# Stick-breaking attention: a block's cast behind the next block's sigmoids on ScalarE, and a fourth buffer for cast probabilities

## The chip, the cores and the metric

The kernel runs on one core of a Trainium2 chip. The metric is the device time of one execution in microseconds (us), as the median of several executions. Five engines work side by side, each through its own queue in order: TensorE (PE in the profile; PEld is its loading of weights), VectorE (DVE), ScalarE (ACT), GpSimd (POOL) and SyncE (SP), which here issues nearly all DMAs. An instruction that waits for a semaphore holds up whatever stands behind it on its engine.

## The reference

One layer of an encoder block with 2048 positions and 1024 columns, batch 1. A normalized input goes through one projection whose columns feed two kinds of attention: four heads of differential attention (two softmax maps each) and eight heads of stick-breaking attention. Both outputs are normalized, projected and added to the input; a gated feed-forward part follows. The part that the change touches is this, with `s < t` strictly:

```python
def stick_breaking_attention(q, k, v):
    """A[t,s] = beta_ts * prod_{s<j<t}(1 - beta_tj), s < t."""
    ...
        z = jnp.einsum('bqhd,bkhd->bhqk', qb, k).astype(jnp.float32) * scale
        log_1mb = jnp.where(mask, jax.nn.log_sigmoid(-z), 0.0)
        rem = lax.cumsum(log_1mb, axis=3, reverse=True) - log_1mb
        a = jnp.where(mask, jnp.exp(jax.nn.log_sigmoid(z) + rem), 0.0)
        return jnp.einsum('bhqk,bkhd->bqhd', a.astype(v.dtype), v)
```

There is no softmax: each weight is a sigmoid times the product of (1 - sigmoid) of all later keys before the query.

## The kernel before, in words

The work is cut into 8 head groups: groups 0 to 3 are one differential head each, groups 4 to 7 are two stick-breaking heads each (m = 0, 1). Queries go in 16 tiles of 128 rows (i), keys in blocks of up to 1024 columns (b) which are computed in chunks of up to 512 (c), the highest first. The projection of the next group (`proj_tile`, `proj_out`, `proj_batch`) is fed in between the attention tiles of the present one by `advance`, and in the last group the output projection (`out_proj`, `post`, `x_ops`) takes that place. The feed-forward part comes afterwards.

A 32-bit number that goes into a matmul is split into two 16-bit halves, high and low, and products take three matmuls. So each block of probabilities is split as well, and transposed by a DMA, since the keys have to lie on the partitions for the product with v.

One stick-breaking block (`stage_a`, L549 to L572) takes, for each chunk: scores on TensorE into a PSUM tile `sc` (L457, four such tiles); on ScalarE the sigmoid of -z into `om` (L563) and the sigmoid of z, `beta` (L566), into the PSUM tile itself or into the tile `be`; on VectorE a running product over the reversed columns (the scan, L568); and on VectorE or GpSimd the product of beta with the shifted scan (L569), which gives the block's probabilities in `be`. `be` and `om` come from the ring `z4` of ZB = 9 tiles (z in the profile). Which engine a part goes to is decided while the program is written out, by `pick`, which keeps a sum of estimated costs for each engine (`load`, `note`).

When the chunks are done, `split_t` (L407) does the split and the transposition:

- a buffer `s16` of 2048 half-precision columns (s in the profile) is taken from a ring of SB = 3; the softmax half uses the same ring, and so does `post` for the operands of the feed-forward part,
- the high half is a cast by `to16`: on ScalarE for stick-breaking (L89),
- the low half is a subtraction (`tt`, L98): on GpSimd for stick-breaking,
- the transposing DMA is issued by SyncE (L412) into `aT`, a ring of AB = 5.

`stage_b` then multiplies the transposed block by v (`pv`, L467), PD = 5 blocks later. An s16 buffer is free when the transpose has landed.

The order on each engine is not the order of the text alone: a scheduler lays out all instructions at build time by priority, by a simulated course of time and by free buffers, and the result is fixed. `queue_behind` (L209) adds edges without a semaphore: an instruction is to stand behind another one on the same engine. So far only the feed-forward part uses it.

The tile `st` (two buffers) holds the split queries and keys before they are transposed, with room for 6 columns of heads; `out_proj` uses the same tag for rows of x (1024 numbers of 32 bit).

Of the kernel before, what the change touches and what calls it, by code (L numbers as in the profile page):

```python
# [11 lines left out]
F32 = mybir.dt.float32  # L12
F16 = mybir.dt.float16
BF16 = mybir.dt.bfloat16
I32 = mybir.dt.int32
AF = mybir.ActivationFunctionType
# [5 lines left out]
S, D, P = 2048, 1024, 128  # L22
# [13 lines left out]
KW = {"A": 1.0, "D": 1.0, "P": 1.0}  # L36
AHEAD = 2
AHN = 0
QB, KB, ZB, AB, SB, PD = 4, 7, 9, 5, 3, 5
XL = (0, 4, 5, 2, 1, 6, 3)  # L40
CU = 3
WE = "AP"
# [17 lines left out]
def block(tc, a, out):  # L60
    nc = tc.nc
    PE, ACT, DVE, POOL, SP = nc.tensor, nc.scalar, nc.vector, nc.gpsimd, nc.sync
    top = ExitStack()
    with top:
# [16 lines left out]
        def level():  # L81
            for k in load:
                load[k] = 0.0

        def to16(dst, src, n, engines="ADP", psum=False):
            cost = {"A": 0.84 * n + 110, "D": (1.05 if psum else 0.53) * n + 70, "P": 1.1 * n + 80}
            e = pick(**{k: cost[k] for k in engines})
            if e == "A":
                ACT.copy(dst, src)  # L89
            elif e == "D":  # L90
                DVE.tensor_copy(dst, src)
            else:
                POOL.tensor_scalar(dst, src, 1.0, 0.0, op0=ALU.mult, op1=ALU.add)
# [15 lines left out]
        def nm(s):  # L109
            uid[0] += 1  # L110
            return f"{s}{uid[0]}"
# [97 lines left out]
        def queue_behind(later, first):  # L209
            for z in later:  # L210
                tc.add_manual_dep(z.ins, first.ins.name, mybir.DependencyInfo(mybir.DependencyClass.NoSync, mybir.DependencyReason.DATA), reason="issue order")
# [46 lines left out]
        pp = pjs.enter_context(tc.tile_pool(name="pp", bufs=2, side="right"))  # L258

        with ExitStack() as ph1:  # L260
# [127 lines left out]
            def proj(g, G, fresh=None):  # L388
                for t in range(NT):
                    if fresh is not None:  # L390
                        feed(t)
                        xt = ahead.pop(0)
                    else:
                        xt = pp.tile([P, 2 * D], F16, tag="xt", bufs=3, name=nm("xt"))
                        SP.dma_start(xt[:], xs[t])
                    if t % 4 == 0:
                        st = pp.tile([P, 6, 4, 2, 64], F16, tag="st", name=nm("st"))
                        v = sp.tile([P, 4, 256], F16, tag="v", bufs=KB, name=nm("v"))
                        raw = pp.tile([P, 4, 256], F32, tag="raw", name=nm("raw")) if g < 4 else None
                    pj = proj_tile(G, xt)  # L400
                    proj_out(g, G, pj, (st, v, raw), t % 4)
                    if t % 4 == 3:
                        proj_batch(g, G, (st, v, raw))
                    yield

            @pri("spl")
            def split_t(src, n, he="ADP", le="DP"):  # L407
                s16 = s16p.tile([P, 2048], F16, tag="s16", bufs=SB, name=nm("s16"))
                to16(s16[:, :n], src, n, he)
                tt(s16[:, n : 2 * n], src, s16[:, :n], ALU.subtract, n, le)  # L410
                aT = sp.tile([P, 16, P], F16, tag="aT", bufs=AB, name=nm("aT"))
                SP.dma_start_transpose(aT[:, : 2 * n // P, :], s16[:, : 2 * n])  # L412
                return aT
# [129 lines left out]
                values(*prev)  # L543

            def sb_attn(g, G):
                last = {}

                @pri("at")
                def stage_a(i, m, b):  # L549
                    L = (i + 1) * 128  # L550
                    n = min(1024, L - 1024 * b)
                    be, om = z4(), z4()
                    if b == i // 8:
                        DVE.memset(om[:, n : n + 1], 8192.0)
                    else:
                        DVE.tensor_copy(om[:, n : n + 1], last[m][:, 0:1])
                    last[m] = om
                    for c in range((n - 1) // 512, -1, -1):
                        lo, hi = 512 * c, min(512 * c + 512, n)
                        w = hi - lo  # L560
                        sc = ps.tile([P, 512], F32, tag="sc", bufs=4, name=nm("sc"))
                        score_chunk(G, sc, i, 2 * b + c, m, w // P, b == i // 8 and hi == n)
                        ACT.activation(om[:, lo:hi], sc[:, :w], AF.Sigmoid, scale=G["nkz"][:])  # L563
                        e = pick(D=1.04 * w + 155, P=2.4 * w + 100)
                        beta = sc[:, :w] if e == "D" else be[:, lo:hi]
                        ACT.activation(beta, sc[:, :w], AF.Sigmoid, scale=G["kz"][:])  # L566
                        ov = om[:, lo:hi][:, ::-1]
                        DVE.tensor_tensor_scan(ov, ov, sc[:, :w], om[:, hi : hi + 1], op0=ALU.mult, op1=ALU.bypass)  # L568
                        (DVE if e == "D" else POOL).tensor_tensor(be[:, lo:hi], beta, om[:, lo + 1 : hi + 1], ALU.mult)  # L569
                        note("A", 1.7 * w + 400)  # L570
                        note("D", 2.08 * w + 200)
                    return n, split_t(be[:, :n], n, "A", "P")  # L572

                ypd = {}

                def stage_b(i, m, b, n, aT):
                    r, k = fq(g, i)
                    if i // k not in ypd:
                        ypd[i // k] = ps.tile([P, 512], F32, tag="yp", name=nm("yp"))
                    yp = ypd[i // k]  # L580
                    pv(G, yp, P * r + 64 * m, aT, b, n, 128 * m, 64, r == 0 and m == 0 and b == i // 8, r == k - 1 and m == 1 and b == 0)
                    if m == 1 and b == 0 and r == k - 1:
                        finish(g, G, i, k, yp)
                        G["fin"] = i + 1

                pend = []
                done = 0
                for i in range(NT):
                    if i % 4 == 0:
                        level()  # L590
                    for b in range(i // 8, -1, -1):
                        for m in range(2):
                            n, aT = stage_a(i, m, b)
                            pend.append((i, m, b, n, aT))
                            if len(pend) > PD:
                                stage_b(*pend.pop(0))
                            done += n // P + CS
                            yield done / (272 + 48 * CS), (i + 1 if b == 0 and m == 1 else i)
                for u in pend:
                    stage_b(*u)  # L600
# [154 lines left out]
            def out_proj():  # L755
                for t in range(NT):
                    mt = pp.tile([P, 2 * D], F16, tag="xt", bufs=3, name=nm("mt"))[:].rearrange("p (k n) -> p k n", k=KT)
                    with tc.high_priority(PRI["wm"]) if PRI["wm"] else nullcontext():
                        mts.append(SP.dma_start(mt, ms[t]))
                    if t in spare:  # L760
                        xf = spare[t].bitcast(F32)
                    else:
                        xf = pp.tile([P, 6, 4, 2, 64], F16, tag="st", name=nm("xf"))[:].rearrange("p c t s e -> p (c t s e)").bitcast(F32)[:, :D]
                    SP.dma_start(xf, x[t * P : (t + 1) * P, :])
                    for h in range(2):
                        po = psj.tile([P, 512], F32, tag="pj", name=nm("po"))
                        for n in range(2):
                            q = 0
                            sl = slice(256 * n, 256 * n + 256)
                            for kt in range(KT):  # L770
                                for xi, wi in ((0, 0), (0, 1), (1, 0)):
                                    PE.matmul(po[:, sl], lhsT=mt[:, kt, P * xi : P * xi + P], rhs=wos[2 * h + n][wi][:, kt, :], start=q == 0, stop=q == 23)  # L772
                                    q += 1
                            xl = xf[:, 512 * h + 256 * n : 512 * h + 256 * n + 256]
                            DVE.scalar_tensor_tensor(xl, po[:, sl], kos[2 * h + n][:], xl, op0=ALU.mult, op1=ALU.add)  # L775
                    note("D", 1400)
                    SP.dma_start(hd[t], xf)
                    if t >= 12:
                        yield
                        continue  # L780
                    post(t, xf)
                    yield
# [459 lines left out]
```

## Time and profile before

| | us |
|---|---|
| Median of 3 runs | 2723.46 (2717.96 to 2725.68) |
| The profiled execution | 2726.11 |
| Its span in the trace | 2724.3 |

The granted TensorE clock was 0.975 on the mean. A profile row of a group of instructions names line, engine, operation and tiles (`out<-in`), then count, busy time, mean duration and the idle time of the engine just before, with what ended it. A row of waits reads "who waited <- for whom: total us, times, longest us". In a row of a window of time stand its length, then the busy time of each engine with the number of instructions in brackets, the granted clock, the mean busy share of the 16 DMA engines, and GB/s. In a timeline each row has start, duration, engine, line and operation; square brackets tell how long the engine stood idle before it and what ended that.

### The profile page before, as it was taken

What the parts mean: (1) busy time and instruction counts of PE and PEld (TensorE: products, weight loads), DVE (VectorE), ACT (ScalarE), POOL (GpSimd) and SP (SyncE); (2) the same over time, 40 slices, a digit from 0 to 9 for tenths busy, and PEclk for the clock granted to TensorE, in tenths of its full rate; (3) what the DMA queues carried; (4) which work ended last, traced back from release to release, by engine and by line L of the source; (5) the groups of instructions that cost most, each with busy time, mean ns of one, the idle gap of its engine ahead of it and who ended that gap; (6) DMA issues with size and microseconds to landing.
All of it is one profiled execution on the core that took longest, in us unless ns stands there. A gap on an engine that the chain in (4) does not pass through costs nothing. (4 is left out here: it accounts for less than half of the span.)

```text
span 2724.3 us, 45559 instructions
## 1 busy us (share of the span) xinstructions
PE 2471.4 (91%) x17084; PEld 1404.6 (52%) x17084; DVE 1945.7 (71%) x3716; ACT 1345.8 (49%) x2483; POOL 1569.3 (58%) x1134
## 2 busy tenths in 40 slices
PE   7998989898888786779888999999999999999998
PEld 4655655555555453557775444444444444444443
DVE  6898979698888988876666877777786544444445
ACT  4665656567878878765644535444352112111121
POOL 2577767667767777765655666575674232323223
PEclk9999999999999997999999999999999999999999
DMA  6788797779999998996797675666749744545534
GB/s 223 205 168 176 149 195 161 177 170 206 208 207 203 205 183 159 205 202 199 203 268 266 237 245 201 220 215 212 251 170 350 279 175 145 224 151 190 208 125 166
DMA packets 649134, 551.92 MB, mean 203 GB/s; under 512 B 506624, under 2 KB 574208, under 8 KB 638672
## 3 DMA queue, kind: packets, MB, share of 16 engines
q1 hardware_dynamic: 647088, 546.92, 73.2%
q8 instruction: 134, 2.20, 0.3%
q0 software_dynamic: 512, 1.36, 0.2%
q10 hardware_dynamic: 1312, 0.72, 0.1%
q14 instruction: 88, 0.72, 0.1%
HBM read 265.27 MB, written 151.52 MB: 153 GB/s over the span
## 5 line engine op out<-in xcount | busy, mean ns | idle before, releaser
L329 PE MATMUL pj<-w,xt 128*128 128x384 f16 x3072 | 570.1, 333 | 26.3 <-DVE st L339 10.8
L98 POOL TENSOR_TENSOR s<-z,s 128x1024 f16<-128x1024 f32 (+7 forms) x288 | 477.5, 1667 | 99.3 <-ACT s L89 94.8
L329 PEld LDWEIGHTS <-xt 128*128 128x128 f16 x3072 | 298.5, 100 | 233.8 <-issue 38.2
L568 DVE TENSOR_TENSOR_SCAN z<-z,sc 128x512 f32<-128x512 f32 (+3 forms) x320 | 352.9, 1112 | 81.4 <-ACT sc L566 39.3
L1048 PE MATMUL pd<-wd,act 128*128 128x512 f16 x1848 | 405.3, 379 | 3.9 <-DVE hs L1054 2.4
L457 PE MATMUL sc<-kT,qT 128*128 128x512 f16 (+3 forms) x1280 | 339.6, 357 | 51.7 <-DVE z L568 16.2
L467 PE MATMUL yp<-v,aT 128*128 128x64 f16 (+1 forms) x4896 | 279.6, 207 | 91.5 <-DMA aT<-s 90.4
L467 PEld LDWEIGHTS <-aT 128*128 128x128 f16 x4896 | 242.2, 101 | 181.9 <-DMA aT<-s 120.2
L98 POOL TENSOR_TENSOR act<-cg,act 128x512 f16<-128x512 f32 x117 | 166.3, 1434 | 239.4 <-ACT act L1006 133.1
L950 PEld LDWEIGHTS <-wg 128*128 128x128 f16 x1848 | 181.1, 98 | 222.0 <-issue 7.9
L1048 PEld LDWEIGHTS <-act 128*128 128x128 f16 x1848 | 180.6, 98 | 222.7 <-issue 4.8
L950 PEld LDWEIGHTS <-wu 128*128 128x128 f16 x1848 | 181.9, 99 | 219.0 <-issue 6.5
L98 POOL TENSOR_TENSOR hs<-hs,cu 128x512 f32<-128x512 f32 x132 | 166.9, 1269 | 220.9 <-DVE hs L1054 76.0
L98 POOL TENSOR_TENSOR fst<-fst 128x512 f32<-128x512 f32 x97 | 182.6, 1883 | 161.3 <-DVE wd L224 89.9
L1054 DVE SCALAR_TENSOR_TENSOR hs<-pd,c,hs 128x512 f32<-128x512 f32 x192 | 141.6, 748 | 155.6 <-PE pd L1048 151.9
L89 ACT CAST s<-z 128x384 f16<-128x384 f32 (+7 forms) x216 | 171.6, 800 | 133.5 <-DMA aT<-s 104.5
L563 ACT ACTIVATE z<-sc,c 128x512 f32<-128x512 f32 (+3 forms) x320 | 207.0, 650 | 25.7 <-PE sc L457 18.5
L569 POOL TENSOR_TENSOR z<-z,z 128x512 f32<-128x512 f32 (+3 forms) x148 | 151.5, 1027 | 100.7 <-DVE z L568 85.6
L772 PE MATMUL po<-wo,mt 128*128 128x256 f16 x1536 | 180.1, 276 | 20.2 <-DVE xf L775 11.2
L1006 ACT CAST act<-cg 128x512 f16<-128x512 f32 x132 | 81.1, 616 | 218.1 <-DVE cg L1012 173.6
L950 PE MATMUL pm<-X,wg 128*128 128x512 f16 x792 | 179.7, 380 | 0.0
L950 PE MATMUL pm<-X,wu 128*128 128x512 f16 x792 | 179.4, 379 | 0.0
(237 smaller groups left out, 4139.3 us busy)
## 6 DMA issues: line engine op xcount, KB each, us to landing
xt<-xs SPq DMA_DIRECT2D x112, 512.0 KB, 4.2
hs<-hd SPq DMA_DIRECT2D x96, 512.0 KB, 4.4
hd<-hs SPq DMA_DIRECT2D x80, 512.0 KB, 4.4
split<-wg SPq DMA_DIRECT2D x11, 1792.0 KB, 11.3
split<-wu SPq DMA_DIRECT2D x11, 1792.0 KB, 10.4
split<-wd SPq DMA_DIRECT2D x11, 1792.0 KB, 10.5
wg<-split SPq DMA_DIRECT2D x11, 1792.0 KB, 7.2
wd<-split SPq DMA_DIRECT2D x11, 1792.0 KB, 8.9
```

What stands on the lines that cost most here:

```text
L89: ACT.copy(dst, src)
L98: (DVE if e == "D" else POOL).tensor_tensor(dst, a_, b_, op)
L329: PE.matmul(pj[:, :384], lhsT=xv[:, xi, kt, :], rhs=G["w"][:, wi, kt, :], start=n == 0, stop=n == 23)
L457: PE.matmul(sc[:, : 128 * w].rearrange("p (t n) -> p t n", n=P), lhsT=G["q"][i // 4][:, 2 - 2 * o + m, i % 4, :], rhs=G["k"][q][:, m, 0:w, ...
L467: PE.matmul(yp[:, y0 : y0 + wd], lhsT=aT[:, a_, :], rhs=v[:, v_ : v_ + wd], start=start and j == 0 and q == 0, stop=stop and j == nb - 1 a ...
L563: ACT.activation(om[:, lo:hi], sc[:, :w], AF.Sigmoid, scale=G["nkz"][:])
L568: DVE.tensor_tensor_scan(ov, ov, sc[:, :w], om[:, hi : hi + 1], op0=ALU.mult, op1=ALU.bypass)
L569: (DVE if e == "D" else POOL).tensor_tensor(be[:, lo:hi], beta, om[:, lo + 1 : hi + 1], ALU.mult)
L772: PE.matmul(po[:, sl], lhsT=mt[:, kt, P * xi : P * xi + P], rhs=wos[2 * h + n][wi][:, kt, :], start=q == 0, stop=q == 23)
L950: PE.matmul(ps_[:].rearrange("p (t n) -> p t n", n=P), lhsT=wv[:, wo, wi, 128 * kt : 128 * kt + 128], rhs=X[xo][:, :, xi, kt, :], start=st ...
L1048: PE.matmul(po[:], lhsT=act[:, ao, xi, 128 * j : 128 * j + 128], rhs=W["d"][:, wo, wi, :], start=start and u == 0 and q == 0, stop=u == nu ...
L1054: DVE.scalar_tensor_tensor(dst, po[:], kd[:], src, op0=ALU.mult, op1=ALU.add)
```

## The change

Three things are changed together. The ring of s16 buffers has four buffers in place of three. Its 4 KB on each partition come from `st`, which gets room for 4 columns of heads in place of 6. And `stage_a` keeps the cast of each block in `held_cast`; in the next block of the same group, once its sigmoids are written out, that cast is queued behind the last of them (`second`) on ScalarE. The last block of a group gets no such edge.

```diff
-QB, KB, ZB, AB, SB, PD = 4, 7, 9, 5, 3, 5
+QB, KB, ZB, AB, SB, PD = 4, 7, 9, 5, 4, 5
...
+        casts16 = []
+
         def to16(dst, src, n, engines="ADP", psum=False):
...
             if e == "A":
-                ACT.copy(dst, src)
+                casts16.append(ACT.copy(dst, src))
...
-                        st = pp.tile([P, 6, 4, 2, 64], F16, tag="st", name=nm("st"))
+                        st = pp.tile([P, 4, 4, 2, 64], F16, tag="st", name=nm("st"))
...
             def sb_attn(g, G):
-                last = {}
+                last, held_cast = {}, []
...
-                        ACT.activation(beta, sc[:, :w], AF.Sigmoid, scale=G["kz"][:])
+                        second = ACT.activation(beta, sc[:, :w], AF.Sigmoid, scale=G["kz"][:])
...
-                    return n, split_t(be[:, :n], n, "A", "P")
+                    if held_cast:
+                        queue_behind([held_cast.pop()], second)
+                    aT = split_t(be[:, :n], n, "A", "P")
+                    held_cast.append(casts16[-1])
+                    return n, aT
...
-                        xf = pp.tile([P, 6, 4, 2, 64], F16, tag="st", name=nm("xf"))[:].rearrange("p c t s e -> p (c t s e)").bitcast(F32)[:, :D]
+                        xf = pp.tile([P, 4, 4, 2, 64], F16, tag="st", name=nm("xf"))[:].rearrange("p c t s e -> p (c t s e)").bitcast(F32)[:, :D]
```

## The prediction

> **What bounds the kernel now.** I read the page first, then the windows by stage, then the waits of the stick-breaking stage, then ScalarE's own order of work. Stages were cut by where the sigmoids of stick-breaking run (third row, 612 to 1377 us).
>
> ```profile
> span 2724.3 us, 45559 instructions
> PE 2471.4 (91%) x17084; PEld 1404.6 (52%) x17084; DVE 1945.7 (71%) x3716; ACT 1345.8 (49%) x2483; POOL 1569.3 (58%) x1134
> ```
> ```profile
> L563 ACT ACTIVATE z<-sc,c x320: 359/688/903, 611.9 to 1376.9; 128x512 f32<-128x512 f32 x88, 128x128 f32<-128x128 f32 x24, 128x256 f32<-128x256 f32 x24, 128x384 f32<-128x384 f32 x24
> ```
> ```profile
> core 0: us, PE busy (x) PEld busy (x) DVE busy (x) ACT busy (x) POOL busy (x), PEclk, DMA share, GB/s
> 0.00:610.00 610.00, 537.51 (x4068) 343.42 (x4069) 505.18 (x1460) 355.28 (x897) 393.55 (x301) 0.98 0.78 180
> 610.00:800.00 190.00, 165.89 (x1677) 106.98 (x1676) 158.67 (x314) 146.31 (x274) 140.54 (x102) 0.96 1.07 209
> 800.00:1200.00 400.00, 316.95 (x3316) 201.76 (x3311) 334.32 (x612) 316.51 (x590) 294.99 (x225) 0.92 0.97 194
> 1040.00:1080.00 40.00, 23.89 (x287) 14.38 (x287) 35.16 (x53) 35.34 (x62) 32.10 (x23) 0.80 0.75 130
> 1200.00:1400.00 200.00, 169.49 (x1848) 143.34 (x1847) 134.77 (x193) 113.76 (x187) 124.22 (x84) 0.97 0.78 199
> 1400.00:2724.00 1324.00, 1281.59 (x6189) 609.07 (x6186) 812.76 (x1141) 413.94 (x541) 615.97 (x424) 0.99 0.59 215
> ```
>
> Over the whole span TensorE is busiest (91%). From 1400 us on the feed-forward part is its own (97%) and has no part in this change. Between 610 and 1200 us no engine is full: in 800 to 1200 VectorE has 84%, TensorE and ScalarE 79% each, GpSimd 74%. So it is waits that set the pace there, and this view of the waits in 610 to 1200 us says which:
>
> ```profile
> ACT s L89 <- DMA aT<-s: 75.6, 55, 3.6
> POOL s L98 <- ACT s L89: 74.2, 57, 5.0
> ...
> DVE z L568 <- ACT sc L566: 34.3, 34, 2.3
> DVE z L568 <- ACT z L566: 30.8, 25, 3.9
> ```
>
> The columns are total us, times, longest. ScalarE's greatest idle time, 75.6 us, comes before the cast (L89), which waits until a transpose of an earlier block has landed: it needs one of the three s16 buffers. Everything behind that cast on ScalarE stands too, so VectorE's scan waits 65.1 us for sigmoids and GpSimd's subtraction 74.2 us for the cast. One turn of the ring, on ScalarE and then on GpSimd:
>
> ```profile
> 1006.17 1.04 ACT L89 CAST s<-z 128x1024 f16<-128x1024 f32 x1 [2.08 <-DMA aT<-s]
> ...
> 1007.76 0.30 ACT L89 CAST s<-z 128x128 f16<-128x128 f32 x1 [0.26 <-DMA aT<-s]
> ...
> 1012.17 0.30 ACT L89 CAST s<-z 128x128 f16<-128x128 f32 x1 [0.51 <-DMA aT<-s]
> ...
> 1016.04 1.99 ACT L89 CAST s<-z 128x1024 f16<-128x1024 f32 x2 [2.83 <-DMA aT<-s]
> ```
> ```profile
> 1007.34 2.13 POOL L98 TENSOR_TENSOR s<-z,s 128x1024 f16<-128x1024 f32 x1 [1.84 <-ACT s L89]
> ```
>
> The buffer taken at 1006.17 is free again at 1016.04, 9.87 us later, for the third cast after it. A third of that is 3.3 us a block. The transposes of 800 to 1200 us, one a block, are
>
> ```profile
> L412 SPq DMA_TRANSPOSE aT<-s x119: 1184/1739/6477, 797.9 to 1199.6; - x119
> ```
>
> so 400 / 119 = 3.4 us a block. The pace is the one that the ring allows: a bound of its own, beside engines that are four fifths busy.
>
> **The change part by part.** No instruction is added or removed. The buffers: st loses two of six columns that nothing writes (proj_out fills st[:, 0:4]), 2 buffers x 2 KB a partition, which pays for one s16 buffer of 4 KB; cost nothing, since the same DMAs read the same columns.
>
> *The order.* Each stick-breaking cast is put behind the last sigmoid (L566) of the next block. Is it not there already?
>
> ```profile
> 1053.35 0.36 ACT L563 ACTIVATE z<-sc,c 128x128 f32<-128x128 f32 x1
> ...
> 1055.10 0.69 ACT L563 ACTIVATE z<-sc,c 128x512 f32<-128x512 f32 x1 [0.20 <-PE sc L457]
> ...
> 1056.25 0.69 ACT L563 ACTIVATE z<-sc,c 128x512 f32<-128x512 f32 x1
> ...
> 1057.39 0.70 ACT L563 ACTIVATE z<-sc,c 128x512 f32<-128x512 f32 x1
> 1057.96 0.71 ACT L566 ACTIVATE z<-sc,c 128x512 f32<-128x512 f32 x1
> ...
> 1059.68 1.40 ACT L89 CAST s<-z 128x640 f16<-128x640 f32 x2
> ```
>
> The first two rows are the 640 columns of block 12, second head, the next two the 1024 of the following block; only then come the two casts of 640, those of both heads. So the first cast already stands behind the sigmoids of two later blocks. Matching the widths of all sigmoids and casts to the loop in this way, from the first cast to the last,
>
> ```profile
> 626.99 0.30 ACT L89 CAST s<-z 128x128 f16<-128x128 f32 x1
> ...
> 1382.06 1.04 ACT L89 CAST s<-z 128x1024 f16<-128x1024 f32 x1 [1.87 <-DVE z L569]
> ```
>
> 173 of the 188 casts that get the new edge satisfy it now. Of the 15 others, 9 lie after 1225 us, where the output projection shares ScalarE. With three buffers the edges would thus move almost nothing, and I put them at 0 by themselves. They matter as a floor: a free buffer lets the build's scheduler draw casts forward, and the edge stops them one block back. What is queued behind a held cast: GpSimd's subtraction, the transpose on SP's queue and then TensorE's products five blocks later (PD = 5), so the few us have cover; 9 casts of the last stage lose some of it, bounded by one landing wait each way, 9 x 1.4 = 12 us (75.6 / 55 = 1.4), and I take 0.
>
> *The fourth buffer.* A cast now waits for the landing four blocks back: 9.87 / 4 = 2.5 us a block in place of 3.3, so the pace of 3.4 us no longer touches it. Upper end of the gain in 610 to 1200 us: VectorE loses all 65.1 us of waiting for sigmoids and is 492.99 / 525 = 94% busy. Lower end of the gain: 0. Between them stands the one stretch where the ring does not bite, 1040 to 1080 us, whose waits for the transposed blocks are
>
> ```profile
> who waited for it (us, times):
> ...
>   ACT s L89: 0.9, 1
> ```
>
> There VectorE has 35.16 of 40 us, 88%, and that is what I take as reached elsewhere: what is late next is VectorE itself, through the score tiles that TensorE waits for. In 800 to 1200 us: 334.32 / 0.879 = 380, a gain of 20. In 610 to 800 us the same sum gives 158.67 / 0.879 = 180.5, a gain of 9.5, but the DMA share there is 1.07, and more transposes in flight meet a queue that is already working; I take 0. In 0 to 610 us the softmax half uses the same ring, mostly with casts on GpSimd, with
>
> ```profile
> ACT s L89 <- DMA aT<-s: 19.1, 6, 5.3
> ```
>
> at most 19 us; VectorE (83%) and TensorE (88%) are busy around it, and I take 0. In 1200 to 1400 us ScalarE waits for the ring
>
> ```profile
> ACT s L89 <- DMA xcd<-x: 12.0, 6, 4.8
> ACT s L89 <- DMA aT<-s: 6.0, 1, 6.0
> ```
>
> 18 us, with TensorE at 85% and ScalarE at 57%; again 0, with 18 as its end. Sum: -20 us. The profiled execution took 2726.11 us (span 2724.3 and 1.8 around it), 2.65 above the median of the runs, 2723.46. Against the median: 2723.46 - 20 = 2703.5, say 2704.
>
> The DMA share is the row that speaks loudest against this sum:
>
> ```profile
> q1 hardware_dynamic: 304267, 116.26, 99.8%
> ```
>
> It is that of 610 to 1200 us: by it the 16 engines are full, and a fourth buffer only lengthens their queue. The Trainium skill, Perfetto Trace Analysis, section Identifying the Most-Contended Engine, holds that occupancy misleads for DMA, because there are 16 engines, and that the rate of bytes should be read instead. This trace agrees so far that the share reaches 1.07 in 610 to 800 us, so 1.00 is no ceiling, and that GB/s moves between 194 and 209 from stage to stage. By the share the sum would be 0 us, by the page's rule the 20 us stand.
>
> **The rivals.**
>
> *The transposes are the bound (no change).* If the DMA engines serve no more than now, landings come later by as much as casts come earlier, and the time stays at 2723, give or take 6. For it: the share of 1.07 and 0.97 in the two windows. Against it: 0.75 in 1040 to 1080 us, with blocks still flowing.
>
> *A new wait on the product (slower).* With a free buffer the cast can be drawn forward to just behind the next block's sigmoids, and then waits on ScalarE's in-order queue for its own product (L569), which needs a scan and a product after the last sigmoid:
>
> ```profile
> L568 DVE TENSOR_TENSOR_SCAN z<-z,sc 128x512 f32<-128x512 f32 x188 | 238.0, 1273 | 44.1 <-ACT sc L566 20.9 <-ACT z L566 20.6
> L569 POOL TENSOR_TENSOR z<-z,z 128x512 f32<-128x512 f32 x95 | 104.6, 1103 | 61.7 <-DVE z L568 54.4 <-DVE m L195 2.6 <-DVE z L556 1.8
> ```
>
> 1.27 + 1.10 = 2.4 us at the least, against four sigmoids of the next block that take 2.3 us (1055.10 to 1057.39 is four starts). There is no slack. ScalarE has 400 - 316.5 = 83.5 us idle in 800 to 1200 us, 0.70 us for each of the 119 casts; it is the bound as soon as the mean wait of a cast passes that. At 0.85 us it needs 316.5 + 101 = 418 us: 18 us slower, 2741. Against it: the cast is seldom pulled that far if the scheduler's picture of VectorE is true, and now this wait ends almost no idle time.
>
> *The whole wait goes (faster by much more).* VectorE to 94%: 2723 - 65 = 2658 at the end, some 2672 if two thirds of the way past my sum come. For it: 610 to 800 us and the two outer stages, which I took at 0. Against it: the densest 40 us that I found have VectorE at 35.88 of 40, 90%, not 94:
>
> ```profile
> 880.00:920.00 40.00, 33.43 (x368) 21.53 (x367) 35.88 (x73) 30.07 (x54) 32.00 (x20) 1.00 1.08 222
> ```
>
>
> **How the numbers follow.** Forecast, 2704 (2692 to 2714): 0.43. No change by the DMAs: 0.20. New wait, slower: 0.23. The much greater gain: 0.14. Within 0.3% (8 us) is what a measurement of this kernel cannot tell from no change. Faster 0.43 + 0.14 = 0.57, same 0.20, slower 0.23. The range must leave out no more than 0.2: from 2668, which keeps nearly all of the great gain, to 2738, which keeps the no-change case and the milder half of the slower one.
>
> **What would show it.** Right: the row of ScalarE's cast waiting for the transposes falls from 75.6 us to under 25 in the stick-breaking stage, VectorE's waits for L566 fall from 65.1 by some 20, VectorE's share in that stage rises towards 88%, and the last sigmoid comes 15 to 25 us sooner than 1377. Wrong by the DMAs: the median from issue to landing of the transposes grows and the landing waits stay. Wrong by a new wait: rows of L89 waiting for L569, now nearly absent, of tens of us. The prediction fails altogether if the scheduler, with another buffer to plan with, lays out the softmax half or the last 200 us otherwise, for which no row here gives a price.

## The result, and the profile after

The change made the kernel slower: median 2738.6 us (2734.73 to 2740.2) against 2724.53 (2717.96 to 2725.68) in four executions of each, a ratio of 1.005 with a 95% interval of 1.0036 to 1.0064. The forecast was 2704, in 2668 to 2738. The kernel before had medians of 2727.85 to 2729.2 in the later comparisons, so below the ratios are to be compared, not the times.

First the page after:

```profile
span 2737.4 us, 45588 instructions
PE 2478.5 (91%) x17084; PEld 1409.6 (51%) x17084; DVE 1957.9 (72%) x3716; ACT 1344.8 (49%) x2483; POOL 1564.3 (57%) x1134
```

The span is 13.1 us longer. The counts of each engine are the same; only the order differs (the 29 instructions more are semaphore instructions). Where the time is lost shows in the transposes, whose rows give count, min/median/max of one in ns, and the first and last start. All 288 of them, before and after:

```profile
L412 SPq DMA_TRANSPOSE aT<-s x288: 1167/1784/6477, 113.8 to 1388.8; - x144
```
```profile
L414 SPq DMA_TRANSPOSE aT<-s x288: 1167/1780/7727, 112.7 to 1401.6; - x144
```

The first 96, which are the softmax half, before and after:

```profile
L412 SPq DMA_TRANSPOSE aT<-s x96: 1169/1772/5368, 113.8 to 631.7; - x96
```
```profile
L414 SPq DMA_TRANSPOSE aT<-s x96: 1169/1662/4889, 112.7 to 637.9; - x96
```

The last transpose is issued 12.8 us later, and 6.2 of that are there already at the end of the softmax half, where no cast has an edge. Counted on in this way, the three full groups of stick-breaking, up to the 240th transpose, took 488.2 us before and 490.9 after, the last group 268.9 and 272.9. From there to the first matmul of the feed-forward part it is 64.5 and 68.5, and that part takes 1266.5 and 1262.8, to the end of VectorE's last instruction. The sum is 6.2 + 2.7 + 4.0 + 4.0 - 3.7 = 13.2 us.

The waits of 610 to 1200 us after, as in the prediction:

```profile
PEld L469 <- DMA aT<-s: 78.3, 63, 5.4
...
POOL s L100 <- ACT s L91: 65.2, 39, 7.0
PE yp L469 <- DMA aT<-s: 57.8, 47, 5.3
ACT s L91 <- DMA aT<-s: 29.3, 20, 3.9
DVE z L570 <- ACT sc L568: 25.2, 25, 4.6
...
DVE z L570 <- ACT z L568: 15.1, 17, 3.7
```

The cast's wait for a landing fell from 75.6 us to 29.3, GpSimd's wait for the cast from 74.2 to 65.2, and the scan's two waits for sigmoids together from 65.1 to 40.3. The two rows of TensorE waiting for transposed blocks stood at 69.0 and 51.8 before:

```profile
PEld L467 <- DMA aT<-s: 69.0, 57, 4.1
...
PE yp L467 <- DMA aT<-s: 51.8, 45, 3.7
```

They are now 78.3 and 57.8, so some of the wait seems to have gone from the cast to the product with v. The windows after:

```profile
610.00:800.00 190.00, 164.05 (x1585) 104.29 (x1584) 160.18 (x318) 141.95 (x264) 137.63 (x99) 0.96 0.99 204
800.00:1200.00 400.00, 318.16 (x3331) 202.35 (x3327) 326.06 (x597) 309.89 (x582) 290.09 (x224) 0.90 0.94 192
```

VectorE has 326.06 of 400 us, 82%, where 88% was forecast and 84% was before. And the sigmoids (L563 before):

```profile
L565 ACT ACTIVATE z<-sc,c x320: 359/687/968, 615.4 to 1390.6; 128x512 f32<-128x512 f32 x88, 128x128 f32<-128x128 f32 x24, 128x256 f32<-128x256 f32 x24, 128x384 f32<-128x384 f32 x24
```

The last one starts 13.7 us later than before, not 15 to 25 sooner. So the wait was taken away and the time did not follow. The experiments had to answer two questions: why the full groups gain nothing, and what costs the 13 us.

### The profile page after: what moved, and what is told of

The parts are those of the page before. It is cut to its first block, busy times and chain, and to the rows that moved or that the text cites. A ratio compares the mean times of both kernels' runs of the same rounds, so it can differ in the third digit from the quotient of the medians.

```text
span 2737.4 us, 45588 instructions
## 1 busy us (share of the span) xinstructions
PE 2478.5 (91%) x17084; PEld 1409.6 (51%) x17084; DVE 1957.9 (72%) x3716; ACT 1344.8 (49%) x2483; POOL 1564.3 (57%) x1134
## 5 line engine op out<-in xcount | busy, mean ns | idle before, releaser
L100 POOL TENSOR_TENSOR s<-z,s 128x1024 f16<-128x1024 f32 (+7 forms) x288 | 469.8, 1643 | 80.8 <-ACT s L91 77.6
L494 DVE TENSOR_SCALAR_CACHE_REDUCE z<-sc,c 128x512 f32<-128x512 f32 (+3 forms) x256 | 160.5, 647 | 27.1 <-PE sc L459 25.6
```

The source lines that it names most:

```text
L100: (DVE if e == "D" else POOL).tensor_tensor(dst, a_, b_, op)
L494: DVE.tensor_scalar(z[:, lo : lo + f], sc[:, :f], kz_d[:], None, op0=ALU.mult, op1=ALU.max, accum_out=mx[:, m, nx : nx + 1])
```

## Experiments: the parts of the change

Stage times below are counted from the transposes as above, one profile each. How well one profile tells a stage: two kernels whose built order in the full groups is the same (e1 and h1, below) took 493.4 and 488.8 us there. Differences of up to some 5 us in a stage of one kernel therefore say nothing, and of the terms above only that of the softmax half is more. A profiled execution also lies up to 5 us from its kernel's median (h1: 2736.09 against 2741.34 us; f1: 2729.46 against 2734.35), so stage times need not add up to the ratios. Short diffs are against the kernel after, those of f3 and f4 against the kernel before.

**e1: the edges alone** (three buffers).

```diff
-QB, KB, ZB, AB, SB, PD = 4, 7, 9, 5, 4, 5
+QB, KB, ZB, AB, SB, PD = 4, 7, 9, 5, 3, 5
...
-                        st = pp.tile([P, 4, 4, 2, 64], F16, tag="st", name=nm("st"))
+                        st = pp.tile([P, 6, 4, 2, 64], F16, tag="st", name=nm("st"))
```

> The order edges alone: ring of three s16 buffers and the wide st tile as before. In the built order the products with v stand 6.38, 7.58 and 6.19 blocks behind the scores in the three full stick-breaking groups (before 6.44, 6.31, 6.52; changed kernel 5.96, 6.06, 5.96). Theory A (the pace of a group is the time from a block's scores to the landing of its transpose, divided by the blocks that TensorE's order leaves for it, and the fourth buffer shortened that distance): within 5 us of before, 2719 to 2729, the second group no slower than before. Rival B (the edges hold the casts back and cost the time): 2733 or more. Rival C (the loss starts in the softmax half, through the shared ring): within 4 us of before, 2720 to 2728.

2734.51 us, ratio 1.0023 (1.0011 to 1.0035). Softmax half 635.2, full groups 493.4, last group 276.4. The total lies in the range of rival B, the edges; h1 and f2, below, ask whether they cost it by holding casts.

**e2: the buffer alone** (no edges).

```diff
-                    if held_cast:
-                        queue_behind([held_cast.pop()], second)
```

> The fourth buffer and the narrow st tile without the edges. The distance is 5.71, 6.02 and 5.98 blocks. Theory A: slower than before like the changed kernel, 2732 to 2745. Rival B (edges): back at before or faster, 2705 to 2726. Rival C (softmax half): 2730 to 2740, with some 6 us lost by the end of the softmax half.

2729.0 us, ratio 1.0003 (0.999 to 1.0017). Softmax half 638.6, full groups 486.1, last group 270.9: without any edge the fourth buffer already brings nothing. The time that the ring's wait took isn't to be had by the ring alone. Neither the buffer alone (+0.03%) nor the edges alone (+0.23%) cost what both together do (+0.5%).

**e3: the fourth buffer for stick-breaking only**, under a tag of its own that each fourth block takes; the softmax half keeps its three (SB = 3 again). All edges stay.

```diff
-            def split_t(src, n, he="ADP", le="DP"):
-                s16 = s16p.tile([P, 2048], F16, tag="s16", bufs=SB, name=nm("s16"))
+            def split_t(src, n, he="ADP", le="DP", fourth=False):
+                s16 = s16p.tile([P, 2048], F16, tag="s16x" if fourth else "s16", bufs=1 if fourth else SB, name=nm("s16"))
...
-                    aT = split_t(be[:, :n], n, "A", "P")
+                    turn[0] += 1
+                    aT = split_t(be[:, :n], n, "A", "P", turn[0] % 4 == 0)
```

> As the changed kernel, but the fourth buffer has a tag of its own that only every fourth stick-breaking block takes; the softmax half and the output stage keep three. The distance is 6.29, 6.81 and 6.42 blocks. Theory A: about before, 2716 to 2728, since the distance is that of before. Rival C (softmax half): the 6 us of the softmax half come back, the stick-breaking groups stay as in the changed kernel, 2730 to 2735. Rival B (edges): 2733 or more.

2736.52 us, ratio 1.0033 (1.0021 to 1.0046). The softmax half is back at 633.1, as rival C had it, but the last group takes 278.1 and the total is in the range of rival B.

**f1 and f2: where the edges are.** f1 is the change without the edges of the last group, f2 the kernel before with those alone.

```diff
-                    if held_cast:
+                    if held_cast and g < NG - 1:
```

> The changed kernel without the edges of the last stick-breaking group, the one beside the output projection; the built order of the three full groups stays that of the changed kernel. Theory E (the edges cost where they truly move casts, the 11 casts of the last group that stood ahead of the next block's sigmoids): 5 to 10 us faster than the changed kernel, at most 3 us over before in the ratio, 0.999 to 1.001. Rival F (the edges cost in the full groups, or the whole is a matter of another order everywhere): ratio 1.003 to 1.006 as in the changed kernel.

> The kernel before (ring of three, wide st) with the edges in the last stick-breaking group alone; all else is laid out as before. Theory E: 4 to 9 us slower than before, ratio 1.0015 to 1.0035, the loss standing between the last transpose of the third group and the first feed-forward matmul. Rival F: ratio 0.999 to 1.001.

f1: 2734.35 us, 1.0022 (1.001 to 1.0034). f2: 2727.43 us, 0.9996 (0.9984 to 1.0008). So the last group's edges, 11 of which weren't met before, cost nothing when they are added to the kernel before; with f2 that group took 266.5 us. Taken from the whole change, the same edges gave 0.28% (1.0022 against 1.005, intervals that don't touch), and f1 lies between its two forecasts. A fixed cost of holding those casts would show in both.

## Experiments: what bounds the full groups

**e5: products later.** After the change TensorE waits more for landings, and in the built order the products stand 6.0 blocks behind the scores of their own block, against 6.4 before. If the pace were the time from scores to product over that distance, a longer distance would free it. e5 queues the first product of a block behind the scores of the block seven later, in the full groups.

```diff
+                        if after is not None:
+                            queue_behind([mm], after)
+                            after = None
...
-                            if len(pend) > PD:
-                                stage_b(*pend.pop(0))
+                            if len(pend) > (7 if g < NG - 1 else PD):
+                                stage_b(*pend.pop(0), scored[0] if g < NG - 1 else None)
```

> As the changed kernel, but in the three full stick-breaking groups the first product of a block with v is queued on TensorE behind the scores of the block seven later. The distance is 7.31, 7.25 and 7.02 blocks. Theory A: TensorE stops waiting for the landing of the transposes, the three groups take 10 to 20 us less in all than in the changed kernel, 2718 to 2729. Rival D (DMA engines or VectorE are full anyway): no change from the changed kernel, 2735 to 2742. Rival B and C: also no change from the changed kernel.

2740.25 us, ratio 1.0041 (1.0025 to 1.0058). The waits in 640 to 1110 us, kernel after and then e5:

```profile
PEld L469 <- DMA aT<-s: 67.8, 55, 3.5
...
PE yp L469 <- DMA aT<-s: 49.6, 41, 3.0
...
PE sc L459 <- DVE z L570: 11.3, 15, 2.0
...
PE sc L459 <- DVE z L571: 5.6, 5, 2.1
```
```profile
PEld L471 <- DMA aT<-s: 23.5, 14, 5.6
...
PE yp L471 <- DMA aT<-s: 19.7, 12, 5.4
PE sc L461 <- DVE z L575: 15.3, 25, 1.0
PE sc L461 <- DVE z L576: 11.9, 10, 2.0
```

TensorE's two rows of waiting for landings (a weight load and its matmul, which may wait at the same time) fell from 117.4 to 43.2 us and the full groups still took 488.2 us. The scores wait longer for VectorE (16.9 to 27.2 in the two rows); that is a part of it, and where the rest went isn't shown. That theory fell. Twice now a wait of tens of us went and the time stayed, so the next runs take work away from one suspect at a time, and then from two.

**f3, f4, g1, g2, f5: one suspect less, and two.** f3 transposes half the columns of a block (the low half, which then stands in for the high half in the products), f4 scans half the columns, g2 does both, g1 is f4 with the ring of four and no edges, f5 has a third of the matmuls in the projection of the stick-breaking groups. All five leave out work that the result needs, or part of its precision; they serve for their times alone.

```diff
-                SP.dma_start_transpose(aT[:, : 2 * n // P, :], s16[:, : 2 * n])
+                SP.dma_start_transpose(aT[:, : n // P, :], s16[:, n : 2 * n]) if half else SP.dma_start_transpose(aT[:, : 2 * n // P, :], s16[:, : 2 * n])
...
-                        DVE.tensor_tensor_scan(ov, ov, sc[:, :w], om[:, hi : hi + 1], op0=ALU.mult, op1=ALU.bypass)
+                        DVE.tensor_tensor_scan(ov[:, : w // 2], ov[:, : w // 2], sc[:, : w // 2], om[:, hi : hi + 1], op0=ALU.mult, op1=ALU.bypass)
```

> The kernel before, but in stick-breaking only the low half of each block is transposed and used for all three products (the high half is left out of the result); the cast and the subtraction stay, the DMA work of a block is half. Three full groups took 488 us with a ring of three or four and with TensorE's distance at 6 or 7 blocks. Theory G (the DMA engines, 99.8% by their share, set that pace): the three groups take 440 us or less, the kernel 2680 or less. Rival H (VectorE sets it): 478 us or more. Theory A or the ring: some 10 to 25 us less, since landings come 1 to 2 us sooner: 463 to 478.

> The kernel before, but each scan runs over half the columns of its chunk (the other half is left unscanned); VectorE has some 140 us less to do in the three full groups. Rival H (VectorE sets the pace of 488 us): the three groups take 440 us or less. Theory G (DMA engines): 478 us or more.

> Scans over half the columns (the rest is left unscanned) together with the fourth buffer, no edges. The three full groups took 488 us before, 486 with the fourth buffer, 494 with half scans. Theory J (two bounds stand side by side, the ring with the landing of transposes, and VectorE with the score tiles it holds; taking away one leaves the other): 470 us or less. Rival G (the DMA engines alone): 484 us or more.

> Half transposes and half scans together (the high half of each block and half of each scan are left out), ring of three, no edges. Half transposes alone gave 474 us for the three full groups, half scans alone 494. Theory J: 450 us or less. Rival L (TensorE, with its granted clock near 0.93 there, or ScalarE sets the pace): 465 us or more.

> The kernel before, but the projections for the stick-breaking groups take one matmul in place of three (the products with the low halves are left out), so TensorE has some 47 us less in each of the three full groups and the same DMAs. Theory J (the ring with the landings, and VectorE): the three groups take 475 us or more. Rival L (TensorE sets the pace): 440 us or less.

| kernel | the three full groups, us | against before |
|---|---|---|
| before | 488.2 | |
| e2, ring of four | 486.1 | -2 |
| f4, half scans | 494.1 | +6 |
| g1, half scans and ring of four | 473.8 | -14 |
| f3, half transposes | 473.8 | -14 |
| g2, half scans and half transposes | 446.9 | -41 |
| f5, a third of the projection | 484.8 | -3 |

(One execution each: f3 2700.69, f4 2707.12, g1 2710.38, g2 2664.09, f5 2742.32 us in all.) The windows of 640 to 1110 us, of before, f4, g1, f3 and g2:

```profile
640.00:1110.00 470.00, 383.99 (x4031) 242.39 (x4029) 396.17 (x714) 378.40 (x691) 348.34 (x259) 0.93 1.02 199
```
```profile
640.00:1110.00 470.00, 380.97 (x3980) 239.82 (x3977) 301.55 (x709) 375.94 (x687) 344.46 (x259) 0.93 0.97 195
```
```profile
640.00:1110.00 470.00, 395.40 (x4191) 251.25 (x4190) 311.05 (x740) 382.35 (x703) 360.80 (x268) 0.93 1.03 205
```
```profile
640.00:1110.00 470.00, 391.94 (x4181) 248.21 (x4179) 409.81 (x737) 386.80 (x712) 355.79 (x268) 0.94 0.70 149
```
```profile
640.00:1110.00 470.00, 404.66 (x4350) 259.37 (x4348) 325.91 (x784) 406.52 (x758) 377.90 (x286) 0.95 0.74 158
```

In f4 VectorE (the third busy time) drops from 396 to 302 us of 470 and nothing is won: the transposes' path holds the same pace. Its scan and cast wait longer in these 470 us than they did with whole scans (31.4 and 60.5 us):

```profile
DVE z L568 <- ACT sc L566: 83.2, 68, 5.1
...
ACT s L89 <- DMA aT<-s: 68.1, 46, 6.4
```

The fourth buffer, worth 2 us with VectorE at 84%, is worth 494.1 - 473.8 = 20 us where VectorE is at 64 to 66% (g1 against f4; the forecast for two bounds had been 470 or less). That is the size of the forecast's gain; it needs room on VectorE. And half scans, worth nothing alone, add 27 us to the half transposes (473.8 to 446.9). The two savings alone come to -14 and +6, together to -41. So, as far as one profile each can show it, two bounds stand side by side at nearly the same pace: the path of a block through cast, subtraction and transpose with its ring, and VectorE. Taking away one shows the other. Half the transposes bring only 14 us although the DMA share falls to 0.70 with f3, so the DMA engines are no bound of their own either; in this the trace agrees with what the prediction cited of the Trainium skill, Perfetto Trace Analysis (Identifying the Most-Contended Engine). f5 leaves TensorE at 68% (its row stands in the last section) and wins 3 us, though at a lower clock. No run takes work from ScalarE or GpSimd; but in g2 these two and TensorE did all their instructions of the full groups in 446.9 us, so the work of none of the three alone sets the 488 us.

All of these orders differ from one another too, and another order alone can be worth 10 us in the full groups (k3, below). So the 27 and the 41 us are clear of that, the 20 of the ring less so, the 14 hardly.

## Experiments: what a single edge costs

**h1 and h2: one edge.** An edge that the kernel before meets already has nothing to hold up. In its full groups only four aren't met, and each of these casts stands ahead by 1.0 to 1.3 us. So h1 takes the kernel before and adds one of the four, in the first full group, whose cast starts at 738.3 us and stands ahead by 1.0 us (h2: one in the second).

```diff
-                    if held_cast:
+                    if held_cast and (g, i, m, b) == (4, 12, 1, 0):
                         queue_behind([held_cast.pop()], second)
```

> The kernel before (ring of three, wide st) with a single edge: the cast of tile 12, first head, block 0 of the first stick-breaking group behind the next block's sigmoids. It stood ahead of one of them by 1.0 us. In the built order all three full groups come out as with all edges (6.38, 7.58, 6.19 blocks). Theory K (an edge costs nothing by holding its cast; it makes the scheduler draw up another order for all that follows, and orders differ by a few tenths of a per cent): ratio 1.001 to 1.004, like all edges without the fourth buffer (1.0023). Rival F (the cost is that of held casts, so a single one costs nothing): 0.999 to 1.001.

> The kernel before with another single edge, in the second stick-breaking group (tile 12, first head, block 1). The first group keeps its order; the third comes out at 7.29 blocks in place of 6.52. Theory K: the ratio may fall on either side, 0.996 to 1.004, and differs from that of the other single edge by more than the interval. Rival F: 0.999 to 1.001, the same as the other.

h1: 2741.34 us, ratio 1.0046 (1.0033 to 1.006). h2: 2734.16 us, 1.0019 (1.0006 to 1.0033). One edge of 188, which moves one cast by about 1 us, costs as much as the whole change (a little more than the 1.004 that was expected at most). The order of the instructions in the traces says how: TensorE's first 5224 of 17084 matmuls, up to 743 us, come in h1 as before, then the order differs; and up to the 8894th, at 1189 us, the order in h1 is that in e1 with all its edges. The scheduler lays out by a simulated course of time; one edge shifts one choice, and later ones are drawn anew. h1's full groups take 488.8 us, as before; its last group, in which it has no edge at all, takes 276.9 against 268.9.

## Experiments: where the fourth buffer goes

k1 and k2 have e3's separate buffer, k1 with no edge and k2 with those of the last group; k3 gives the fourth buffer to the softmax half alone, without edges.

```diff
-                    if held_cast:
+                    if held_cast and g == NG - 1:
                         queue_behind([held_cast.pop()], second)
-                    aT = split_t(be[:, :n], n, "A", "P")
+                    turn[0] += 1
+                    aT = split_t(be[:, :n], n, "A", "P", turn[0] % 4 == 0)
```

This is k2; in k1 the `if` and its line are gone.

> The fourth buffer in stick-breaking alone, in a tag of its own, and no edges. Theory M: the softmax half ends at 631 to 635 us, as before. Theory J (ring and VectorE are two bounds side by side): the three full groups take 484 to 489 us, no real gain. Theory K (what is left is the chance of another order): ratio anywhere in 0.997 to 1.003. A version that beats both kernels would be below 0.998.

> As the one above, with the edges in the last stick-breaking group alone, where with three buffers they cost nothing (0.9996). The full groups have the order of the one above. Theory K: the two differ only after 1120 us, by anything up to 8 us either way; ratio 0.996 to 1.004. Rival F (held casts cost): slower than the one above.

> The kernel before, narrow st, no edges, with the fourth buffer in the softmax half alone (every fourth block there takes a tag of its own); stick-breaking and the output stage keep three. The order of the softmax half comes out as in the changed kernel. Theory M (with a free buffer the softmax half's casts are drawn forward and then wait for their own product, and that costs that half some 5 us): the last transpose of the softmax half is issued at 636 us or later, before at 631 to 635 in the kernels with three buffers; ratio 1.001 to 1.005. Rival N (the later end of that half in the kernels with four buffers came from elsewhere, such as addresses): 631 to 635.

| kernel | ratio (95%) | softmax half to, us | full groups | last group |
|---|---|---|---|---|
| k1 | 0.9972 (0.996 to 0.9983) | 633.7 | 486.1 | 265.5 |
| k2 | 0.9969 (0.9957 to 0.9981) | 632.0 | 489.5 | 265.2 |
| e3 = k2 and the other edges | 1.0033 (1.0021 to 1.0046) | 633.1 | 489.4 | 278.1 |
| k3 | 1.0061 (1.0043 to 1.0079) | 635.6 | 498.3 | 272.7 |

k1 (2721.68 us) and k2 (2720.28) beat both kernels, by 0.3%. k3 is the slowest of all, outside the 1.005 that was expected of it at most, and its softmax half falls between the two forecasts (636 or later, 635 at most).

All six kernels with four buffers in the softmax half end it at 635.6 to 644.1 us (mean 639.0), eleven with three at 631.2 to 635.2 (mean 633.0): 6 us. These are not 17 separate orders. TensorE's first 4100 matmuls come in one order in all six and in another in all eleven; the two part at the 890th, near 168 us. So the 6 us are the difference of these two orders, well measured; that a fourth buffer would cost as much in any other order isn't shown. (f5 is left aside: it has three, ends at 649.8, and leaves out part of a projection that runs there.) The waits of 120 to 630 us show what differs. Before, beside the 19.1 us of the cast for a landing that the prediction shows:

```profile
POOL s L93 <- DVE z L516: 80.7, 30, 8.8
...
ACT y L425 <- PE yp L467: 18.2, 8, 5.4
...
ACT s L89 <- DVE z L516: 2.9, 3, 1.9
```

After, and k3 behind it:

```profile
POOL s L95 <- DVE z L518: 91.5, 32, 8.7
...
ACT y L427 <- PE yp L469: 34.7, 12, 7.7
...
ACT s L91 <- DVE z L518: 21.7, 9, 4.5
```
```profile
ACT y L427 <- PE yp L469: 32.8, 12, 7.5
ACT s L91 <- DVE z L520: 21.8, 9, 4.5
```

The wait for the landing is gone (19.1 us), and in its place the cast waits 21.7 us for VectorE to finish the probabilities that it casts (2.9 before), and ScalarE's reading of the results (y) 34.7 us for TensorE's products (18.2). GpSimd's casts wait longer for the same (80.7 to 91.5). The rows fit a cast that, with a buffer free, is laid out where its input isn't there yet. k1, with three buffers there, has the rows of before:

```profile
ACT y L427 <- PE yp L469: 23.3, 8, 6.9
ACT s L91 <- DMA aT<-s: 19.4, 6, 5.3
```

The share of k3's loss in this half is small, though; 10 us of it lie in the full groups, which have three buffers and no edges, as before: another redrawn order.

## Why the prediction was wrong

- *The ring and its pace of 3.3 us a block*: right as an observation, since the landing wait fell by 46 us (75.6 to 29.3; I had named under 25), and the fourth buffer brought 20 us in the full groups once VectorE had room (g1 against f4).
- *What is late next*: the step that failed. The sum took VectorE to 88% because it had that in 1040 to 1080 us, where the ring didn't bite. It came to 82%. The term of -20 us measured +2.7 with the change and -2.1 with the buffer alone, over the three full groups. What the runs showed in its place is that VectorE holds the pace already at 82 to 84%, beside the path of a block (f4, g1, g2). I read one stretch of 40 us as what the stage reaches without the ring. But it is among the four densest of the fourteen such stretches between 640 and 1200 us; VectorE's shares in them go from 78% (the row below) to the 90% of 880 to 920 us that the prediction shows.

```profile
680.00:720.00 40.00, 35.98 (x359) 22.65 (x357) 31.01 (x58) 31.94 (x57) 27.18 (x21) 1.00 1.10 202
```

  I had not asked what else was absent there either. The windows of the kernel before, with the projection's matmuls (L329) alone, 640 to 1110 us, then that stretch, then 880 to 920 us:

```profile
640.00:1110.00 470.00, 199.03 (x1092) 104.38 (x1092) 0.93 1.02 199
```
```profile
1040.00:1080.00 40.00, 0.00 (x0) 0.00 (x0) 0.80 0.75 130
```
```profile
880.00:920.00 40.00, 20.26 (x117) 11.20 (x118) 1.00 1.08 222
```

  The projection's matmuls, 42% of the stage's time, weren't running in it. That this is what keeps VectorE under 88% elsewhere isn't shown: it has 90% in 880 to 920 us with the projection running, and f5, with a third of these matmuls, wins 3 us. Why VectorE's mean stops at 82 to 84% stays open.
- *The edges at 0*: in the sense meant, right: 173 were met before, and f2, with the 47 of the last group, is at 0.9996. But adding one that wasn't met redraws the order after it, and that cost 0.19 to 0.64% (h2, e1, h1, and e3 against k2) or nothing (f2, and k2 against k1). The prediction named the scheduler as that which could make it fail altogether and gave it no price; the price was there to be measured with one edge.
- *The softmax half at 0*: +6 us. I had an upper end for its gain and none for its loss. The wait is that of the slower rival (the cast drawn forward to wait for its own input), in the half where I had not looked for it. In stick-breaking itself, 610 to 1200 us, it stayed small, as the prediction's own objection had it: 12.2 us in two rows, against 0.9 before (GpSimd's product). The rival needed 0.70 us for each of 119 casts, so its 2741 us lies near the result by luck:

```profile
ACT s L91 <- POOL z L571: 6.8, 9, 1.6
...
ACT s L91 <- DVE z L571: 5.4, 3, 3.8
```

- *1200 to 1400 us at 0*: the last group took 4.0 us more, which one profile can't tell from nothing; but over the kernels that leave no work out it goes from 265.2 to 278.1. The four at 275 and more (e1, e3, h1, h2) have in common that some full group has an edge while the softmax half has three buffers; edges of the last group itself go with 266.5 (f2), 265.2 (k2) and 278.1 (e3). What in an order makes the one or the other isn't settled. The prediction's two rows for this stage are those of 1225 to 1395 us; over the whole 200 us the cast's wait for transposes is 10.9 us, so the end of that term was 23 us and not 18.
- *The DMA rival*: it had the full groups right, which didn't change, but not by its cause. The signs named for it were a longer time from issue to landing, and landing waits that stay; the former stayed at its median (4.5 us before, 4.4 after) and the cast's wait fell. The DMA share fell too:

```profile
q1 hardware_dynamic: 301204, 114.58, 95.1%
```

- *The greater gain*: against it spoke VectorE at 90% at most; the runs put the obstacle earlier.

So of the 13 us, 6 lie in the softmax half, whose order with four buffers is the slower of two in 17 profiles. e2 has that order too and comes out even, at 1.0003, while k1, without it, is 0.31% faster than e2. The other 7 us are spread over the later stages; of them the experiments show only that a redrawn order alone moves them as much. Their cause stays open. Whether the 0.3% of k1 and k2 come from the buffer or from a lucky order stays open. That e3 lost 0.64% against k2 by edges in groups that then took the same time (489.5 and 489.4 us) speaks for not trusting so small a gain to last through the next edit.

## What to carry to other kernels

A wait of 75 us at the head of the list is a gain only if the next bound has room. With all engines near 80% busy, test two suspects together before pricing one: here -2 us with the ring alone, -20 with room on VectorE. Where a scheduler lays out the program, size what a new order is worth with an edit that does next to nothing (one edge, one cast moved by 1 us): here +0.46%, nearly two thirds of the 20 us that were sought. And a buffer added to a ring that two stages share can reorder both; try it under a name of its own, for the one stage that waits.

## What the runs showed of the hardware that was not expected

In f5 TensorE has fewer matmuls to do, and the granted clock is lower. The window of 640 to 1110 us:

```profile
640.00:1110.00 470.00, 318.70 (x3299) 188.79 (x3297) 402.65 (x710) 375.88 (x691) 348.62 (x262) 0.82 0.93 187
```

0.82 at 68% busy, against 0.93 at 82% before (383.99 of 470); over the whole span 0.940 against 0.975. The window of 1040 to 1080 us in the prediction (0.80 at 60%) is of the same kind. So part of what is saved on TensorE is lost to the clock: in 640 to 1110 us the 328 score matmuls of 512 columns took 405 ns each before and, as many of them, 466 ns in f5:

```profile
L457 PE MATMUL sc<-kT,qT 128*128 128x512 f16 x328 | 102.2, 405 | 22.0 <-DVE z L568 7.9 <-DVE z L554 5.7 <-DVE z L556 4.8
```
```profile
L457 PE MATMUL sc<-kT,qT 128*128 128x512 f16 x328 | 120.3, 466 | 57.9 <-DVE z L569 18.9 <-DVE z L554 16.8 <-DVE z L568 13.6
```

The Trainium skill, TensorE: Matmul & The Clock Gate, Part 1, says that the clock is throttled by default and that recent activity of the array releases it; the rows of the windows agree in direction.
